# A transformer block on one core: first loads issued from two engines, first weight cast moved to VectorE, first matmuls in another order

## The chip, the cores and the metric

The kernel runs on one core of a Trainium2 chip. The core has a matmul engine (TensorE, "PE" in the profile, with its weight loads listed apart as "PEld"), VectorE ("DVE"), ScalarE ("ACT"), GpSimd ("POOL") and a queue engine ("SP") that issues most DMA transfers. ACT and POOL can issue transfers too. The metric is the time of one execution on the device in microseconds (us). Lower is better.

## The reference

One block on a sequence of 512 tokens with 1024 channels, float32. The input is normalised, projected by one wide matrix, and the projection feeds a convolution branch and a state-space branch; both are gated, mixed, normalised and followed by a gated feed-forward network:

```python
def reference(x, mix_pre_g, w_in, ...):
    h = rms_norm(x, mix_pre_g[i])
    proj = h @ w_in[i]
    u_glu = proj[..., :OFF_Z]
    z = proj[..., OFF_Z:OFF_XBC]
    xbc = proj[..., OFF_XBC:OFF_DT]
    dt_raw = proj[..., OFF_DT:OFF_GATE]
    gates = jax.nn.sigmoid(proj[..., OFF_GATE:] + gate_b[i])
    g_conv, g_ssm = jnp.split(gates, 2, axis=-1)
    conv_out = conformer_conv_branch(u_glu, ...)
    ssm_out = ssd_branch(z, xbc, dt_raw, ...)
    mixed = (g_conv * conv_out + g_ssm * ssm_out) @ w_out[i]
    x = x + rms_norm(mixed, mix_post_g[i])
    h = rms_norm(x, ffn_pre_g[i])
    gt, up = jnp.split(h @ w_gate_up[i], 2, axis=-1)
    f = (jax.nn.silu(gt) * up) @ w_down[i]
    x = x + rms_norm(f, ffn_post_g[i])
    return x
```

The change touches only the beginning: the first part of `h @ w_in`, whose columns `u_glu` are made of a half "val" and a half "glu".

## The kernel before, in words

Activations are held channel-major: a tile has 128 channels on the partitions and the 512 tokens along the free dimension, so that the 1024 channels are 8 k steps. Weights come in pieces of 128x1024 float32 (512 KB), each holding, for 128 output columns, the 8 k steps side by side, 128 columns per step.

**Split products.** To keep float32 precision, every operand is split into an upper and a lower part in the faster matmul format. For weights, `w_part` (line 167) first casts the raw piece to the upper part `whi` on ACT (L169), then takes the lower part `wlo = raw - whi` on DVE (L176), or for some later pieces through a DMA. For the input, `ehi` is the scaled input on ACT (L334) and `elo` the remainder on DVE (L325). A product is three matmuls: upper weight by upper input, lower weight by upper input, upper weight by lower input.

**The start.** While the first transfers are under way, PE runs 8 matmuls on a zeroed tile (`WARM = 8`, L293; each shows in the trace as two passes, 16 rows in all). ACT loads its function table and makes a one-column copy (`warm`, L290). SP issues all first transfers, in this order: `x0g` (the first 128 channels of the transposed input, with the gains beside it), the first quarter (256 columns, two k steps) of the weight pieces 0, 1 and 2 (`raw0`, `raw1`, `raw2`, L308), the second input tile `xT1`, the second quarters of the three pieces, `xT2`, `xT3`, the second halves of the three pieces, then `xT4` to `xT7` and whole pieces from there on. SP's transfers signal on 8 semaphores in turn; a transfer that comes round to a semaphore waits until the one before it on the same semaphore has landed.

**The first matmul group** (L514 to L518) makes three results at once, `pv0` (val 0), `pg0` (glu 0) and `pv1` (val 1), with one accumulator bank each. The loop runs over the 8 k steps, in each over the three results, and for each result over the three products:

```python
for k in range(NK):
    for ps, (wh, wl) in zip(three, ws):
        c = slice(k * P, (k + 1) * P)
        in_order(pe.matmul(ps, wh[:, c], ehi[k], start=k == 0, stop=False))
        pe.matmul(ps, wl[:, c], ehi[k], start=False, stop=False)
        mark["pe"] = pe.matmul(ps, wh[:, c], elo[k], start=False, stop=k == NK - 1)
```

k steps 0 and 1 need the first quarters of the weights, steps 2 and 3 the second quarters, steps 4 to 7 the halves. Beside this, ACT also squares each input tile (`sq`, L346) and DVE adds the squares (`ssq`, L347) for the norm, whose factor is applied to the first results later (`rb`).

**Order.** Instructions that are not tied by `in_order` are placed by a scheduler that works on its own estimates, so moving one changes its neighbours on ACT and DVE. Each engine then runs its own list strictly in that order, and waits on semaphores for the others. After the first group the kernel goes on for about a thousand microseconds with the other projections, the two branches, the mixing and the feed-forward network; nothing of that is touched.

## Time and profile before

| | |
|---|---|
| runs | 1023.64, 1025.57, 1022.51 us; median 1023.64 |
| the profiled execution | 1022.63 us, of which the span of the core's instructions is 1020.9 us |
| TensorE busy | 1007.8 us, 99% of the span |
| VectorE, ScalarE, GpSimd busy | 843.7, 616.6, 105.6 us |
| moved by DMA | 155.55 MB, 152 GB/s over the span |

Times in the views count from the start of the span. A row of the order of time gives the start, the time taken, engine, line, operation, output and inputs, and in brackets the idle time of the engine before it and what released it. "SPq" and "ACTq" are transfers being issued by SP and ACT. A matmul row's length includes the time through the array; back to back, the next starts before the last has ended, so the distance of their starts is what one costs.

### The profile page before, as it was taken

How to read it: one execution, taken by the hardware profiler on the slowest of the kernel's cores; microseconds unless marked ns; L12 is line 12 of the kernel's file. 1: busy time of each engine (PE TensorE's matmuls, PEld its weight loads, DVE VectorE, ACT ScalarE, POOL GpSimd, SP SyncE). 2: the span in 40 equal slices, each digit the busy share in tenths (PEclk: the TensorE clock that was granted, in tenths of full speed). 3: DMA queues.
4: the chain of work that ended last, by engine and by line, in shares of the span. 5: the costliest groups of instructions: out<-in, count | busy, mean ns of one | idle time of the engine just before them, and what ended most of it. 6: DMA issues, size and time to landing. Idle time of an engine off the chain costs nothing.

```text
span 1020.9 us, 15946 instructions
## 1 busy us (share of the span) xinstructions
PE 1007.8 (99%) x6181; PEld 881.9 (86%) x6181; DVE 843.7 (83%) x1227; ACT 616.6 (60%) x1034; POOL 105.6 (10%) x131
## 2 busy tenths in 40 slices
PE   9999999999999999999999999999999999999997
PEld 7898889888888888888888889889999999988885
DVE  7899977878696879578987889688998788799974
ACT  7645775667666656573552676466676565678542
POOL 0011202120121012101010110011000000001000
PEclk9999999999999999999999999999999999999999
DMA  8567645646554465455352455634656455469622
GB/s 287 157 161 197 185 101 145 182 99 170 148 150 118 128 183 145 113 148 153 81 145 64 123 177 134 221 106 128 207 145 191 120 145 160 129 192 294 196 83 83
DMA packets 44235, 155.55 MB, mean 152 GB/s; under 512 B 5120, under 2 KB 6144, under 8 KB 43136
## 3 DMA queue, kind: packets, MB, share of 16 engines
q1 hardware_dynamic: 30672, 104.66, 30.2%
q0 software_dynamic: 11280, 43.52, 21.8%
q10 hardware_dynamic: 2208, 6.36, 1.7%
q8 instruction: 48, 0.79, 0.3%
q14 instruction: 27, 0.22, 0.1%
HBM read 150.26 MB, written 4.26 MB: 151 GB/s over the span
## 4 chain that ended last, share of the span: by engine, by line
PE 88%; DVE 6%; ACT 2%; issue 1%; DMA 1%; SPq 0%; POOL 0%; ACTq 0%; DVEq 0%; POOLq 0%
PE xy L209 4%; PE xy L211 4%; PE xy L210 4%; PE pso L209 3%; PE pso L210 3%; PE pso L211 3%; PE pz L210 3%; PE pz L211 3%; PE px L211 2%; PE px L209 2%; PE px L210 2%; PE pz L209 2%; PE yv L209 2%; PE yv L210 2%; PE yv L211 2%
## 5 line engine op out<-in xcount | busy, mean ns | idle before, releaser
L467 DVE SCALAR_TENSOR_TENSOR a<-v,prm_t,a 128x511 f32<-128x511 f32 (+15 forms) x240 | 181.4, 759 | 15.5 <-ACT a L464 13.4
L169 ACT CAST whi<-raw 128x1024 fp32r<-128x1024 f32 (+2 forms) x108 | 106.8, 1000 | 131.1 <-PE pso L210 37.5
L176 DVE TENSOR_TENSOR wlo<-raw,whi 128x1024 fp32r<-128x1024 f32 (+2 forms) x67 | 74.9, 1123 | 38.3 <-ACT whi L169 37.6
L174 POOL DMA_DIRECT2D wlo<-in_w x41 | 36.5, 891 | 374.9 <-ACT wlo L173 121.0
L210 PE MATMUL pz<-wlo,hhi 128*128 128x512 f32 (+2 forms) x160 | 56.1, 351 | 0.4 <-DVE wlo L176 0.4
L211 PE MATMUL pz<-whi,hlo 128*128 128x512 f32 (+2 forms) x160 | 56.3, 352 | 0.0
L209 PE MATMUL pz<-whi,hhi 128*128 128x512 f32 (+2 forms) x160 | 55.4, 353 | 0.0
L209 PE MATMUL px<-hhi,whi 128*128 128x512 f32 x128 | 50.2, 392 | 0.0
L209 PE MATMUL pso<-yh,whi 128*128 128x512 f32 x128 | 50.0, 393 | 0.0
L211 PE MATMUL px<-hhi,wlo 128*128 128x512 f32 x128 | 49.8, 389 | 0.0
L210 PE MATMUL px<-hlo,whi 128*128 128x512 f32 x128 | 49.8, 389 | 0.0
L210 PE MATMUL pso<-yl,whi 128*128 128x512 f32 x128 | 49.7, 390 | 0.0
L211 PE MATMUL pso<-yh,wlo 128*128 128x512 f32 x128 | 49.7, 389 | 0.0
L1122 ACT CAST whi_g<-raw 128x1024 fp32r<-128x1024 f32 x40 | 41.3, 1051 | 11.9 <-DVE raw L1161 5.1
L551 DVE SCALAR_TENSOR_TENSOR x<-px,prm_t,x 128x511 f32<-128x511 f32 (+2 forms) x48 | 34.7, 741 | 13.8 <-ACT x L549 13.8
L1127 DVE TENSOR_TENSOR wlo_g<-raw,whi_g 128x1024 fp32r<-128x1024 f32 x34 | 41.1, 1220 | 4.6 <-ACT whi_g L1122 4.5
L173 ACT ACTIVATE wlo<-whi 128x1024 fp32r<-128x1024 f32 x41 | 43.3, 1055 | 0.3
L449 ACT ACTIVATE L<-L,nacs 128x128 f32<-128x128 f32 x128 | 38.8, 389 | 0.5 <-POOL L L442 0.4
L210 PEld LDWEIGHTS pz<-wlo,hhi 128*128 128x128 f32 x160 | 30.2, 188 | 4.5 <-DVE wlo L176 0.7
L209 PEld LDWEIGHTS pz<-whi,hhi 128*128 128x128 f32 x160 | 30.2, 189 | 3.8
L211 PEld LDWEIGHTS pz<-whi,hlo 128*128 128x128 f32 x160 | 30.2, 188 | 3.7
L1122 ACT CAST chi_g<-raw 128x1024 fp32r<-128x1024 f32 x24 | 24.9, 1054 | 10.7 <-DVE raw L1161 4.1
(749 smaller groups left out, 3439.5 us busy)
## 6 DMA issues: line engine op xcount, KB each, us to landing
raw<-in_w SPq DMA_DIRECT2D x182, 512.0 KB, 4.4
wlo<-in_w POOLq DMA_DIRECT2D x41, 512.0 KB, 6.6
L<-scr POOLq DMA_DIRECT2D x8, 1024.0 KB, 7.2
wlo_g<-in_w POOLq DMA_DIRECT2D x11, 512.0 KB, 6.6
clo_g<-in_w POOLq DMA_DIRECT2D x7, 512.0 KB, 5.8
pws<-in_w POOLq DMA_DIRECT2D x8, 256.0 KB, 5.6
pw_raws<-in_w SPq DMA_DIRECT2D x4, 512.0 KB, 6.1
xr<-in_x ACTq DMA_DIRECT2D x4, 512.0 KB, 4.6
```

Source lines behind the costliest of these rows:

```text
L169: act.copy(hi[:, c], src[:, c])
L173: act.activation(lo[:, c], hi[:, c].bitcast(F32), AF.Copy, scale=-1.0)
L174: mark["lo"] = pool.dma_start(lo[:, c], w[n][:, c].bitcast(F32R), accum_op=ALU.add)
L176: mark["wlo"] = dve.tensor_tensor(out=lo[:, c], in0=src[:, c], in1=hi[:, c].bitcast(F32), op=ALU.subtract)
L209: mark["pe"] = pe.matmul(ps, lh, rh, start=start, stop=False, skip_group_check=more)
L210: pe.matmul(ps, lh, rl, start=False, stop=False, skip_group_check=more)
L211: mark["pe3"] = pe.matmul(ps, ll, rh, start=False, stop=stop, skip_group_check=more)
L449: act.activation(L[:, h, c, :], L[:, h, c, :], AF.Exp, bias=nacs[:, c, HG * g + h : HG * g + h + 1])
L467: return dve.scalar_tensor_tensor(out=va[j][:, d:], in0=vs[j][:, : T - d], scalar=col("dw_w", j * KC + KC - 1 - d), in1=va[j][:, d:], op0= ...
L551: dve.scalar_tensor_tensor(out=a[:, d:], in0=ps[:, : T - d], scalar=col("ssm_w", i * KS + KS - 1 - d), in1=a[:, d:], op0=ALU.mult, op1=ALU ...
L1122: a_ = act.copy(hi, src)
L1127: d_ = dve.tensor_tensor(out=lo, in0=src, in1=hi.bitcast(F32), op=ALU.subtract)
```

## The change

- One warm-up matmul fewer (7 instead of 8).
- The first input tile `x0g` is loaded as two transfers, 64 partitions each, one issued by SP and one by ACT. The first quarter of `raw0` is issued by SP, those of `raw1` and `raw2` by ACT. The remaining first transfers stay on SP, in the order that they had. ACT issues its three transfers before it loads its function table.
- The upper part of the first quarter of weight piece 0 is cast on DVE instead of ACT.
- In k step 0 the three upper products (one per result) are issued first, then for each result the two others. The other k steps keep their order, all of it now fixed in program order.

```diff
-WARM = 8
+WARM = 7
...
-    def w_part(n, c):
+    def w_part(n, c, by_dve=False):
         (hi, lo), src = split[n], raws[n]
-        act.copy(hi[:, c], src[:, c])
+        if by_dve:
+            dve.tensor_copy(hi[:, c], src[:, c])
+        else:
+            act.copy(hi[:, c], src[:, c])
...
+    x0g = ssd.tile([P, 3 * GW], F32, tag="yo", name="x0g")
+    for n, (q, h) in enumerate(((nc.sync, slice(0, 64)), (nc.scalar, slice(64, P)))):
+        in_order(q.dma_start(x0g[h, : T + NK], x0[h]))
+    for n, q in enumerate((nc.sync, nc.scalar, nc.scalar)):
+        in_order(q.dma_start(raws[n][:, parts[0]], w[n][:, parts[0]]))
     warm = cp.tile([P, 1], F32, name="warm")
-    act.copy(warm, woken[:, :1])
+    in_order(act.copy(warm, woken[:, :1]))
...
-    def load(c):
-        for n in range(3):
-            in_order(nc.sync.dma_start(raws[n][:, c], w[n][:, c]))
-
-    for k in range(NK):
-        in_order(nc.sync.dma_start(xk[k] if k else x0g[:, : T + NK], xT[k] if k else x0))
-        if k == 0:
-            load(parts[0])
+    for k in range(1, NK):
+        in_order(nc.sync.dma_start(xk[k], xT[k]))
         if k in (1, 3):
-            load(parts[k + 1])
+            for n in range(3):
+                in_order(nc.sync.dma_start(raws[n][:, parts[k + 1]], w[n][:, parts[k + 1]]))
...
         if k in parts:
-            w_part(0, parts[k])
+            w_part(0, parts[k], k == 0)
...
             for k in range(NK):
+                c = slice(k * P, (k + 1) * P)
+                for n in range(3 if k == 0 else 0):
+                    in_order(pe.matmul(three[n], ws[n][0][:, c], ehi[k], start=True, stop=False))
                 for ps, (wh, wl) in zip(three, ws):
-                    c = slice(k * P, (k + 1) * P)
-                    in_order(pe.matmul(ps, wh[:, c], ehi[k], start=k == 0, stop=False))
-                    pe.matmul(ps, wl[:, c], ehi[k], start=False, stop=False)
-                    mark["pe"] = pe.matmul(ps, wh[:, c], elo[k], start=False, stop=k == NK - 1)
+                    if k:
+                        in_order(pe.matmul(ps, wh[:, c], ehi[k], start=False, stop=False))
+                    in_order(pe.matmul(ps, wl[:, c], ehi[k], start=False, stop=False))
+                    mark["pe"] = in_order(pe.matmul(ps, wh[:, c], elo[k], start=False, stop=k == NK - 1))
```

What stands on the engines is seen in three places. The first is SP's list from its beginning; the brackets name the semaphores that a transfer waits for, DMAHW0 to DMAHW7 being those that transfers signal. Before:

```order
L311 DMA x0g_106<-in_x0 128x520
L308 DMA raw0_124<-in_w 128x256
L308 DMA raw1_125<-in_w 128x256
L308 DMA raw2_126<-in_w 128x256
L311 DMA xT1_107<-in_xT 128x512
L308 DMA raw0_124<-in_w 128x256
L308 DMA raw1_125<-in_w 128x256
L308 DMA raw2_126<-in_w 128x256
L311 DMA xT2_108<-in_xT 128x512 [waits DMAHW0_49]
L311 DMA xT3_109<-in_xT 128x512 [waits DMAHW1_49]
```

And after:

```order
L298 DMA x0g_98<-in_x0 64x520
L300 DMA raw0_95<-in_w 128x256
L314 DMA xT1_114<-in_xT 128x512
L317 DMA raw0_95<-in_w 128x256
L317 DMA raw1_96<-in_w 128x256
L317 DMA raw2_97<-in_w 128x256 [waits DMAHW0_49]
L314 DMA xT2_115<-in_xT 128x512 [waits DMAHW1_49]
L314 DMA xT3_116<-in_xT 128x512 [waits DMAHW2_49]
```

Two transfers have left SP's list ahead of `xT1`. The lists of both engines share the 8 semaphores, so the second quarter of `raw2` now comes round to the semaphore of SP's half of `x0g` (DMAHW0) and `xT2` to that of ACT's half (DMAHW1).

The second place is ACT's list from its first cast or scaling of k step 0 on. Before (the table load and the one-column copy stand ahead of it):

```order
L334 ACTIVATE ehi0_114<-x0g_106 128x512
L169 CAST whi_0_152<-raw0_124 128x256
L169 CAST whi_1_154<-raw1_125 128x256
L169 CAST whi_2_158<-raw2_126 128x256
L334 ACTIVATE ehi1_115<-xT1_107,x0g_106 128x512
L169 CAST whi_0_152<-raw0_124 128x256
L346 ACTIVATE sq1_201<-xT1_107 128x512
L169 CAST whi_1_154<-raw1_125 128x256
L169 CAST whi_2_158<-raw2_126 128x256
L334 ACTIVATE ehi2_116<-xT2_108,x0g_106 128x512
```

And after (its half of `x0g` and the first quarter of `raw1` are issued ahead of this):

```order
L300 DMA raw2_97<-in_w 128x256
L302 ACT_TABLE_LOAD
L302 COPY warm_104<-woken_93 128x1
L336 ACTIVATE ehi0_121<-x0g_98 128x512
L172 CAST whi_1_154<-raw1_96 128x256
L172 CAST whi_2_158<-raw2_97 128x256
L336 ACTIVATE ehi1_122<-xT1_114,x0g_98 128x512
L172 CAST whi_0_152<-raw0_95 128x256
L172 CAST whi_1_154<-raw1_96 128x256
L172 CAST whi_2_158<-raw2_97 128x256
L348 ACTIVATE sq1_201<-xT1_114 128x512
L336 ACTIVATE ehi2_123<-xT2_115,x0g_98 128x512
```

The first cast has gone to DVE, and the square `sq1` has moved from between the casts of the second quarters to behind the last of them, directly ahead of `ehi2`. On DVE the moved cast stands first, ahead of `wlo` of piece 0; in DVE's later list two of the additions to `ssq` stand a place or two later.

The third place is PE's list in k step 0, behind the warm-up. Before:

```order
L516 MATMUL pv0_236<-ehi0_114,whi_0_152 128x512
L517 MATMUL pv0_236<-ehi0_114,wlo_0_153 128x512
L518 MATMUL pv0_236<-elo0_122,whi_0_152 128x512
L516 MATMUL pg0_237<-ehi0_114,whi_1_154 128x512
L517 MATMUL pg0_237<-ehi0_114,wlo_1_155 128x512
L518 MATMUL pg0_237<-elo0_122,whi_1_154 128x512
L516 MATMUL pv1_238<-ehi0_114,whi_2_158 128x512
```

And after:

```order
L518 MATMUL pv0_236<-ehi0_121,whi_0_152 128x512
L518 MATMUL pg0_237<-ehi0_121,whi_1_154 128x512
L518 MATMUL pv1_238<-ehi0_121,whi_2_158 128x512
L522 MATMUL pv0_236<-ehi0_121,wlo_0_153 128x512
L523 MATMUL pv0_236<-elo0_129,whi_0_152 128x512
L522 MATMUL pg0_237<-ehi0_121,wlo_1_155 128x512
L523 MATMUL pg0_237<-elo0_129,whi_1_154 128x512
```

The three upper products come first; from k step 1 on the list is the same as before.

More of the change, by code (lines that the diff above doesn't have):

```diff
@@ L293, in block_kernel @@
         in_order(pe.matmul(ps[:, :P], woken, woken, start=True, stop=True))
-    x0g = ssd.tile([P, 3 * GW], F32, tag="yo", name="x0g")
     pre_g = x0g[:, T : T + NK]
```

6 lines of the change are left out of this document (3 added, 3 removed).

## The prediction

> **What bounds the kernel now.** I read the page first, then what PE waits for, then PE's busy time by stretches, then the chain of waits through the first 12 us. The page's busy times and its chain:
>
> ```profile
> PE 1007.8 (99%) x6181; PEld 881.9 (86%) x6181; DVE 843.7 (83%) x1227; ACT 616.6 (60%) x1034; POOL 105.6 (10%) x131
> ...
> PE 88%; DVE 6%; ACT 2%; issue 1%; DMA 1%; SPq 0%; POOL 0%; ACTq 0%; DVEq 0%; POOLq 0%
> ```
>
> PE is busy 99% of the span, so a change at the start can gain only what PE loses at the start. PE's waits (total, times, longest, in us), and PE's busy time by stretches of the start (length, busy, instructions, clock, DMA share, GB/s):
>
> ```profile
> PE xy L209 <- DVE f L1315: 1.3, 1, 1.3
> PE pv L516 <- ACT ehi L334: 0.9, 1, 0.9
> ```
>
> ```profile
> 4.70:9.80 5.10, 5.02 (x19) 1.00 0.91 307
> 9.80:11.90 2.10, 1.15 (x4) 1.00 0.99 350
> 11.90:40.00 28.10, 28.10 (x134) 1.00 0.73 259
> ```
>
> The only wait of PE at the start, 0.9 us, is not in k step 0 but at 9.8 to 10.7, and behind 11.9 PE has no idle time for 28 us: there, an earlier start of PE would not be eaten by another wait. What the wait is made of, from the chain and the order of time:
>
> ```profile
> 4.48 5.42 DMA xT<-in_xT
> ```
>
> ```profile
> 9.27 0.41 ACT L169 CAST whi<-raw 128x256 fp32r<-128x256 f32 x1 [1.07 <-DMA raw<-in_w]
> ...
> 9.92 0.72 ACT L334 ACTIVATE ehi<-xT,x0g 128x512 fp32r<-128x512 f32 x1 [0.25 <-DMA xT<-in_xT]
> ...
> 10.67 0.75 DVE L325 SCALAR_TENSOR_TENSOR elo<-xT,x0g,ehi 128x512 fp32r<-128x512 f32 x1 [0.54 <-ACT ehi L334]
> ...
> 10.69 0.50 PE L516 MATMUL pv<-ehi,whi 128*128 128x512 f32 x1 [0.91 <-ACT ehi L334]
> ...
> 11.48 0.50 PE L518 MATMUL pv<-elo,whi 128*128 128x512 f32 x1
> ```
>
> This is k step 2. `xT2` lands at 9.90 (4.48 + 5.42), ACT scales it from 9.92, PE starts 0.77 us later (10.69), and `elo2`, hence the third product at 11.48, follows 1.56 us behind the start of `ehi2`. From there PE runs without a gap. So the end of the program moves with the start of `ehi2`, and everything that the change does to k steps 0 and 1 lies ahead of that wait. The quantity to work out is when ACT can start `ehi2`.
>
> **The change, part by part.** *Issue.* SP's issues before:
>
> ```profile
> 0.73 0.39 SPq L311 DMA_DIRECT2D x0g<-in_x  x1
> 1.17 1.37 SPq L308 DMA_DIRECT2D raw<-in_w  x3
> 2.58 0.43 SPq L311 DMA_DIRECT2D xT<-in_xT  x1
> 3.05 1.38 SPq L308 DMA_DIRECT2D raw<-in_w  x3
> 4.48 0.91 SPq L311 DMA_DIRECT2D xT<-in_xT  x2
> ```
>
> One issue costs about 0.47 us from start to start. With `raw1` and `raw2` gone to ACT, these two are issued 0.47 us earlier (at 1.17 and 1.64 behind ACT's half of `x0g`), `xT1` and the second quarters of `raw0` and `raw1` 0.94 us earlier. The second quarter of `raw2` would be issued at 3.06 instead of 4.00, but waits for SP's half of `x0g`; the whole of `x0g` landed by 3.67 (ACT's row below), so it is issued by 3.7, 0.3 earlier, and `xT2` by 4.15, also 0.3 earlier.
>
> *Landing.* An earlier issue is an earlier landing only where the transfers wait for the issue. The rate of all transfers from 1.6 to 5.6 us, in 40 slices of 0.1 us:
>
> ```profile
> GB/s 0 166 125 83 42 83 146 187 166 333 395 393 372 320 434 319 318 369 266 277 297 236 246 72 51 51 72 41 51 123 205 277 317 389 338 328 369 328 328 348
> ```
>
> From 3.9 to 4.5 six slices stand at 41 to 72, mean 56, against some 340 on both sides: the transfers have run dry there. That costs 0.6 x (1 - 56/340) = 0.50 us, and the three slices of climb behind it (123, 205, 277) another 0.12: 0.6 us in all. Behind it the rate is full, so `xT2`, 5.42 us under way, stood in line behind bytes. I take it that the earlier issues (0.47 and 0.94 us) fill this hole, so that all later landings come 0.6 us earlier. Unknown is how two issuing queues share the line; the nearest rows are two loads of the same size from either queue:
>
> ```profile
> raw<-in_w SPq DMA_DIRECT2D x182, 512.0 KB, 4.4
> ...
> xr<-in_x ACTq DMA_DIRECT2D x4, 512.0 KB, 4.6
> ```
>
> The ends: 0.2 us later (ACT's loads took 4.6 against 4.4), and 0.94 us earlier (the largest advance of an issue). I take 0.6, since the hole is measured and both advances that could fill it are of its size.
>
> Here stands the rule that speaks against this change. The Trainium skill (DMA: Bandwidth & Descriptors, Issuing engines are not separate DMA queues) says that transfers issued by different engines run on the same 16 DMA engines and interleave, and that only the issue time is saved; its Rules for kernel authors call two transfers to disjoint halves of the partitions not worth it. Taken at its word, splitting `x0g` gains nothing; the trace's hole agrees that issue time is what there is to save, and the case where even that saves nothing is the first rival below.
>
> *ACT.* Its rows at the start:
>
> ```profile
> 0.72 1.28 ACT L290 ACT_TABLE_LOAD   x1 [0.72 <-PEq L1703]
> 2.01 0.19 ACT L290 COPY warm<-woken 128x1 f32<-128x1 f32 x1
> 3.67 0.72 ACT L334 ACTIVATE ehi<-x0g 128x512 fp32r<-128x512 f32 x1 [1.46 <-DMA x0g<-in_x]
> 4.29 0.39 ACT L169 CAST whi<-raw 128x256 fp32r<-128x256 f32 x1
> 5.11 0.41 ACT L169 CAST whi<-raw 128x256 fp32r<-128x256 f32 x1 [0.43 <-DMA raw<-in_w]
> ...
> 6.97 0.39 ACT L169 CAST whi<-raw 128x256 fp32r<-128x256 f32 x1
> 7.27 0.63 ACT L346 ACTIVATE sq<-xT 128x512 f32<-128x512 f32 x1
> 7.80 0.39 ACT L169 CAST whi<-raw 128x256 fp32r<-128x256 f32 x1
> ```
>
> Three issues ahead of the table load take 3 x 0.47 = 1.41 us, so the table load and the copy end at about 3.6 instead of 2.2: just the 1.46 us that ACT idled there. It costs nothing unless `x0g` lands before 3.6; an earlier landing of its halves is then lost. The square that moved is the cost: ACT now does the last cast of the second quarters, then `sq1`, then `ehi2`. A cast costs 0.30 us from start to start (6.97 to 7.27), a square 0.53 (7.27 to 7.80). Before, the last cast waited for `raw2` until 9.27. So `ehi2` starts at the later of the landing of `xT2` and that of `raw2` + 0.83: with unmoved landings max(9.90, 10.10) = 10.10, 0.18 later than the 9.92 of before. With all landings 0.6 earlier it is 9.50, 0.42 earlier. That difference is the sum; the rest costs nothing:
>
> *The cast on DVE*:
>
> ```profile
> L176 DVE TENSOR_TENSOR wlo<-raw,whi 128x256 fp32r<-128x256 f32 x6 | 2.5, 423 | 4.8 <-ACT whi L169 4.8
> ```
>
> ```profile
> L361 DVE TENSOR_SCALAR dg<-ident,nrm 128x128 f32<-128x128 f32 x4 | 0.9, 284 | 1.3 <-POOL nrm L218 1.3
> ```
>
> No such cast of DVE is in the trace: between 0.28 us (one input, half the columns) and 0.42 (two inputs, the same columns); I take 0.4, the row with the same columns. DVE idles 4.8 us ahead of the six `wlo` of this stretch, which hides it. ACT is freed of 0.30 us before 5.11, where it waited for `raw1` anyway.
>
> *PE.* The warm-up's rows, a later product of the same 128x128 shape, and the first real ones and the first of k steps 3 and 4:
>
> ```profile
> L293 PE MATMUL warm_ps<-woken x16: 421/421/581, 1.0 to 4.4; 128*128 128x128 f32 x16
> ```
>
> ```profile
> L367 PE MATMUL prb<-dg,ones x8: 270/275/275, 31.8 to 32.6; 128*128 128x128 f32 x8
> ```
>
> ```profile
> 4.74 0.79 PE L516 MATMUL pv<-ehi,whi 128*128 128x512 f32 x1
> ...
> 6.20 0.39 PE L516 MATMUL pg<-ehi,whi 128*128 128x512 f32 x1
> ...
> 13.21 0.39 PE L516 MATMUL pv<-ehi,whi 128*128 128x512 f32 x1
> ...
> 15.25 0.39 PE L516 MATMUL pv<-ehi,whi 128*128 128x512 f32 x1
> ```
>
> One warm-up matmul is two passes of (4.4 - 1.0)/15 = 0.23: PE is free 0.45 us earlier, at about 4.3. `raw0` was there by 4.29, when ACT cast it without waiting, so DVE has `whi` of piece 0 by 4.7 at the latest, and `ehi0` ends at 4.39: the first product starts at about 4.6, 0.1 earlier, and the upper products fill the 1.46 us that stand between 4.74 and 6.20 with three products instead of the three of one result. All of that ends at k step 2: PE is done with k step 1 earlier and waits longer, about 1.1 us. With the wait at k step 2 gone, the whole of it would be worth at most the 0.45 us of the warm-up matmul. The norm's additions that moved on DVE end long before PE needs them:
>
> ```profile
> 23.35 0.69 DVE L347 TENSOR_TENSOR ssq<-ssq,sq 128x512 f32<-128x512 f32 x1
> ```
>
> ```profile
> L356 PEld LDWEIGHTS pss<-ones,ssq x8: 188/192/192, 25.9 to 26.8; 128*128 128x128 f32 x8
> ```
>
> 1.9 us lie between the last addition's end (24.04) and 25.9.
>
> The profiled execution took 1022.63 us, its span 1020.9; less 0.42 that is 1022.2. The median of the runs is 1.0 above it, so I predict 1023.64 - 0.42 = 1023.2.
>
> **The rivals.** *The landings don't move.* The line is limited by bytes, the hole only shifts. For it: the transfers run at 300 GB/s or more from 4.7 to 11.9, and `xT2` is late by bytes, not by issue. Against it: the hole. Then `sq1` ahead of `ehi2` decides: +0.18, time 1023.8, slower, on one ACT instruction, as soon as the landings come less than 0.18 us earlier. With ACT's loads 0.2 slower it is +0.38, 1024.0.
>
> *The issues bring their whole advance.* Landings 0.94 earlier: `ehi2` at 9.16, 0.76 earlier, time 1022.9. PE, done with k step 1 by about 9.3, would allow it. Against it: `raw2` and `xT2` are themselves issued only 0.3 earlier.
>
> *PE's slow start lasts longer.* The warm-up passes are 0.23 apart, those of `prb` (32.6 - 31.8)/7 = 0.11: PE runs at half rate at first, though the clock column says 1.00, and at full rate from 6.20. If k steps 0 and 1 all ran at half rate, 0.46 instead of 0.23 apart, 18 products from 4.6 would end at 12.9; a k step at full rate takes 2.04 (13.21 to 15.25), so k step 3 would start at 14.9 instead of 13.2: +1.7, time 1025.3. It decides from five half-rate products more than before (1.1 us of wait divided by 0.23). For it: one warm-up fewer. Against: PE's work has no gap over 0.2 us there, and products begin earlier. The Trainium skill (TensorE: Matmul & The Clock Gate, What's actually happening) says the full rate comes after about 3.4 us of sustained activity, in a free-running window, whatever the number of matmuls; by that rule PE gets its full rate at about the same time as before, and a step that misses a window would wait for the next, which is this rival.
>
> **How the numbers follow.** Forecast (landings 0.4 to 0.8 earlier) 0.60; landings not moved 0.22; whole advance 0.10; half rate 0.05; something unseen 0.03. What a measurement of this kernel can tell is about 0.3%, 3.1 us, the spread of the three runs shown. None of the cases reaches it, so: within 0.3% 0.94, slower 0.03 (half rate that lasts beyond k step 3), faster 0.03. The range takes the cases from -0.76 to +0.38 (1022.9 to 1024.0) and adds 1 us on each side, a third of the runs' spread, for a median of few runs: 1021.9 to 1025.0.
>
> **What would show it.** Right: no hole in the rate before 4.5; `ehi2` at about 9.5 with `sq1` just ahead of it; PE's wait at k step 2 longer than 0.9 us, its end at about 10.3; the first product at about 4.6; everything behind shifted by the same 0.4 us. Wrong: `ehi2` later than 9.92, a wait of PE behind k step 2 that was not there, matmuls 0.46 us apart behind 6.2, or ACT waiting for its own two weight quarters past 7.5 (it has 1.9 us there, since `ehi2` needs 2.4 us of ACT's work behind them).

## The result and the profile after

The changed kernel takes 1026.3 us (median of 20 runs, 1024.52 to 1031.67) against 1023.27 us for the kernel before in the same series (20 runs, 1021.47 to 1028.46): a ratio of 1.0031, 95% interval 1.0017 to 1.0045. It is slower by 0.3%, some 3 us; predicted were 1023.2 us and no measurable change. Two further series of the changed kernel gave ratios of 1.0010 [0.9994, 1.0025] and 1.0031 [1.0011, 1.0052] (`after_again` and `after_third` below). The profiled execution took 1025.14 us with a span of 1023.4, against 1022.63 and 1020.9 before: +2.5 us.

The times of every kernel here, the one before too, fall into two heaps some 5 us apart (the last section shows the stage that this comes from), and a median moves with the share of the upper heap. So beside each ratio stands the first quartile of the times less the first quartile of before in the same series, which the upper heap reaches least. For the changed kernel it is +2.75 us (1025.085 less 1022.333).

PE's busy time in the stretches that the prediction spoke of (length, busy, instructions, clock, DMA share, GB/s), after the change:

```profile
4.40:6.40 2.00, 0.00 (x0) 1.00 0.95 293
6.40:9.80 3.40, 3.38 (x8) 1.00 0.92 297
9.80:11.90 2.10, 2.10 (x6) 1.00 0.81 270
11.90:40.00 28.10, 28.10 (x132) 1.00 0.71 249
```

The same stretches of the kernel before:

```profile
4.40:6.40 2.00, 1.93 (x6) 1.00 0.92 305
6.40:9.80 3.40, 3.39 (x15) 1.00 0.87 292
9.80:11.90 2.10, 1.15 (x4) 1.00 0.99 350
```

Two things changed places. PE's idle time, 0.9 us at k step 2 before, is now 2.0 us ahead of the first product. And from 6.4 to 9.8, where PE is busy without a break in both, it gets through 8 products instead of 15: they run at half the rate. The clock column reads 1.00 in all of these rows, so it does not tell: in every trace here the clock records begin with the rise to full rate, and ahead of that record the column shows 1.00. The distance of the starts does tell. PE's own rows after the change:

```profile
6.42 0.77 PE L518 MATMUL pv<-ehi,whi 128*128 128x512 f32 x1 [2.02 <-DVE whi L170]
6.98 0.63 PE L518 MATMUL pg<-ehi,whi 128*128 128x512 f32 x1
...
10.40 0.63 PE L521 MATMUL pv<-ehi,whi 128*128 128x512 f32 x1
...
12.10 0.50 PE L522 MATMUL pg<-ehi,wlo 128*128 128x512 f32 x1
12.44 0.39 PE L523 MATMUL pg<-elo,whi 128*128 128x512 f32 x1
...
13.37 0.39 PE L521 MATMUL pv<-ehi,whi 128*128 128x512 f32 x1
```

From 6.98 to 12.10 the products are 0.43 us apart (12 steps in 5.12 us) and their rows 0.63 long; from 12.44 on they are 0.23 apart and 0.39 long. The last row is the first product of k step 2, which stood at 10.69 before, so PE is 2.68 us late there. The first product is 1.68 late (6.42 against 4.74). The 18 products of k steps 0 and 1 take 6.95 us (6.42 to 13.37), where before they took 5.95 with the wait at their end: 1.00 more. These two make up the 2.68. The norm's matmuls, later on the same engine, start in the kernel before and in the changed one at

```profile
L356 PE MATMUL pss<-ones,ssq x8: 168/250/250, 26.1 to 26.8; 128*128 128x1 f32 x8
```

```profile
L358 PE MATMUL pss<-ones,ssq x8: 169/250/251, 28.4 to 29.1; 128*128 128x1 f32 x8
```

that is 2.3 us later, and the span ends 2.5 us later. The rest of the 2.68 is time that k step 2 lost before and no longer loses: it took 2.52 us (10.69 to 13.21), with its third product waiting for `elo2` until 11.48, and now takes 2.06 (13.37 to 15.43). The norm's row serves below as the mark of what the start has cost. The code behind it is the same in all kernels, but its time is not: from this row to the first `yv` row of the last section it took 709.5 to 712.6 us in the twenty profiles. The mark moves too: two edits that cost nothing in the times, `order_only` and `x_halves`, have it at 25.5, against the 26.1 of the one profile of before. So half a microsecond at the mark of a single execution says little. The chain of waits of the changed kernel, in order of time, says what was late:

```profile
0.73 0.57 SPq L298
...
1.35 4.60 DMA raw<-in_w
...
5.98 0.31 DVE whi L170
...
6.42 0.77 PE pv L518
```

The first quarter of `raw0`, issued 0.18 us after where it stood before (1.35 against 1.17), was under way for 4.60 us and landed at 5.95. Before, ACT had cast it at 4.29. The chain no longer passes through `xT2`. On ACT and DVE one sees that k step 2 was ready long before PE was:

```profile
4.21 0.72 ACT L336 ACTIVATE ehi<-x0g 128x512 fp32r<-128x512 f32 x1 [0.30 <-DMA x0g<-in_x]
...
8.21 0.62 ACT L348 ACTIVATE sq<-xT 128x512 f32<-128x512 f32 x1
...
8.74 0.71 ACT L336 ACTIVATE ehi<-xT,x0g 128x512 fp32r<-128x512 f32 x1
...
9.65 0.75 DVE L327 SCALAR_TENSOR_TENSOR elo<-xT,x0g,ehi 128x512 fp32r<-128x512 f32 x1
```

`ehi2` starts at 8.74 instead of 9.92 and `elo2` ends at 10.40, while PE comes to k step 2 at 13.37. The quantity on which the prediction was built, the start of `ehi2`, improved by 1.18 us, more than the largest case, and no longer mattered.

### The profile page after: what moved, and what is told of

It is laid out like the page before. It is cut to its first block, busy times and chain, and to the rows that moved or that the text cites. A ratio compares the mean times of both kernels' runs of the same rounds, so it can differ in the third digit from the quotient of the medians.

```text
span 1023.4 us, 15945 instructions
## 1 busy us (share of the span) xinstructions
PE 1008.8 (99%) x6179; PEld 883.2 (86%) x6179; DVE 843.1 (82%) x1228; ACT 616.2 (60%) x1033; POOL 105.9 (10%) x131
## 4 chain that ended last, share of the span: by engine, by line
PE 93%; DVE 3%; DMA 1%; issue 1%; ACT 1%; POOL 0%; ACTq 0%; DVEq 0%; POOLq 0%; SPq 0%
PE xy L212 4%; PE xy L213 4%; PE xy L214 4%; PE pz L213 3%; PE pz L214 3%; PE pz L212 3%; PE pso L212 3%; PE pso L213 3%; PE px L214 3%; PE pso L214 3%; PE px L212 3%; PE px L213 3%; PE yv L213 2%; PE yv L212 2%; PE yv L214 2%; PE yd L664 2%
```

## The experiments

Each run is the kernel before or the changed kernel with the edit shown. "Rate up" below is the time of the clock record that puts PE at full rate.

**First series: which half of the change, and is it the warm-up?** Theory: PE starts late and cold, and runs at half rate for so long that PE itself becomes the bound. Rival: the loads are late, and the rate is beside the point.

`after_warm16`, the changed kernel with a long warm-up:

```diff
-WARM = 7
+WARM = 16
```

> The kernel after the change with 16 warm-up matmuls instead of 7, nothing else. Theory 1 (clock): the first weight quarter lands late, PE idles about 2 us behind the warm-up, and therefore runs its first products at half rate up to 12.1 us. With the warm-up reaching into the first product there is no idle time: products from about 6.6 us on at 0.23 us each, no stretch at 0.43, time about 1023 us, 3 us below the 1026.3 of the changed kernel. Theory 2 (landings): the late landings alone cost the time; the warm-up changes nothing, time about 1026 us.

Measured: 1023.97 us, ratio 1.0006 [0.9991, 1.0021], quartile +0.39. The rate was up at 4.02. The first product came at 6.04, but not for want of data: `raw0` had been cast from 4.45 on, and it was the warm-up that lasted until then. For `raw1` and `raw2`, which were late, PE waited 0.20 and 0.38 us. The norm's matmuls started at 26.4. So the longer warm-up alone takes back most of the loss; the 0.3 us left at the mark hold the late data and the length of the warm-up together.

`before_warm4`, the kernel before with a short warm-up (`WARM = 4`):

> The kernel before with 4 warm-up matmuls instead of 8, so that PE idles from about 2.8 us to the first product at 4.7. Theory 1 (clock): the idle time alone, without any change of the loads, brings the stretch at half rate; first products 0.43 us apart up to 9 or 12 us, time 1.5 to 2.5 us above the kernel before, 1025 to 1026. Theory 2 (landings): nothing changes, about 1023.3 us.

Measured: 1023.42 us, ratio 1.0012 [1.0002, 1.0023], quartile +0.62. PE stayed at half rate until 10.26, but the cost expected (1.5 to 2.5 us) did not come: the norm's matmuls started at 26.6, 0.5 late. PE came to k step 2 at 11.61, 0.92 later than before, and passed through it without the 0.46 us that it lost there before. So half rate alone costs little where the data of k step 2 are the bound.

`loads_only`, the changed loads with the rest as before:

```diff
-WARM = 7
+WARM = 8
...
-            w_part(0, parts[k], k == 0)
+            w_part(0, parts[k])
...
-                for n in range(3 if k == 0 else 0):
-                    in_order(pe.matmul(three[n], ws[n][0][:, c], ehi[k], start=True, stop=False))
```

(and the three products of a result one behind the other in k step 0 too).

> Of the change only the loads (two issuing engines, first x tile in halves); 8 warm-up matmuls, the first cast on ACT and the order of products as before. Both theories put the loss on the loads: the first quarter of piece 0 lands near 6 us instead of 4.3, time 2 to 3 us above the kernel before, 1025.3 to 1026.3. A third possibility, that the cast on DVE, the order of the products or the warm-up matmul cost the time, expects about 1023.3.

Measured: 1024.3 us, ratio 1.002 [1.0006, 1.0034], quartile +0.51. Expected were 2 to 3 us; the median stands 1.4 above that of before in its series (1024.3 against 1022.87). In the profile the first product came at 5.15, the rate was up at 5.65 and the norm's matmuls started at 25.5, so that this execution lost nothing at the start. What the loads cost in the other executions was not seen.

`no_loads`, the rest of the change (7 warm-up products, cast on DVE, upper products first) with the loads of before:

```diff
-WARM = 8
+WARM = 7
...
-        act.copy(hi[:, c], src[:, c])
+        if by_dve:
+            dve.tensor_copy(hi[:, c], src[:, c])
+        else:
+            act.copy(hi[:, c], src[:, c])
```

> The change without its loads: 7 warm-up matmuls, the first cast on DVE, upper products first, all first loads issued by SP as before. Theories 1 and 2: within 0.5 us of the kernel before, 1022.8 to 1023.6, first product near 4.7 us, PE still waits at k step 2. The third possibility: about 1026.

Measured: 1023.64 us, ratio 1.0012 [1.0001, 1.0024], quartile +0.66. Its profile shows the mechanism best. PE by stretches, and PE's rows:

```profile
4.00:7.20 3.20, 1.88 (x7) 1.00 0.81 256
7.30:10.60 3.30, 3.30 (x10) 0.54 0.92 309
10.70:14.00 3.30, 3.30 (x15) 0.96 1.05 404
```

```profile
4.38 0.50 PE L519 MATMUL pv<-ehi,whi 128*128 128x512 f32 x1
4.82 0.49 PE L519 MATMUL pg<-ehi,whi 128*128 128x512 f32 x1
6.57 0.50 PE L519 MATMUL pv<-ehi,whi 128*128 128x512 f32 x1 [1.26 <-ACT whi L172]
...
7.15 0.40 PE L524 MATMUL pv<-elo,whi 128*128 128x512 f32 x1
7.39 0.49 PE L523 MATMUL pg<-ehi,wlo 128*128 128x512 f32 x1
7.67 0.63 PE L524 MATMUL pg<-elo,whi 128*128 128x512 f32 x1
...
10.66 0.53 PE L523 MATMUL pg<-ehi,wlo 128*128 128x512 f32 x1
```

The rate was up at 4.12. Then the third upper product waited 1.26 us for `raw2`, the rate fell at 7.53, in the midst of PE's unbroken work, and came back at 10.95. Between these three points lie 3.41 and 3.42 us. The rows fit a rate that is decided at fixed points 3.41 us apart, by how full PE was in the stretch that has just ended (the last section counts this over all profiles); an idle time can then cost a whole such stretch at half rate, later, when nothing is late any more. The Trainium skill (TensorE: Matmul & The Clock Gate, What's actually happening) states such a free-running window of 3413 ns; the trace agrees. The norm's matmuls started at 26.9, 0.8 late, and the wait at k step 2 that was expected was not there: PE came to it at 11.96.

**Second series: which of the loads.** `after_again` is the changed kernel once more.

> The changed kernel once more, to see in a second execution what of its first 13 us repeats. Theory 1 (idle time of PE ahead of late data, then half rate): again a gap of 1 us or more behind the warm-up, and a stretch of products 0.43 us apart, but its length may differ (3 to 6 us), so that the norm's matmuls start between 27 and 29 us against 26.1 in the kernel before; time about 1026. Rival (the first profile was a chance): no gap, no such stretch, norm's matmuls near 26.

Measured: 1024.98 us, ratio 1.001 [0.9994, 1.0025], quartile +1.53; rate up at 10.54, norm's matmuls at 27.8. None of its 10 runs lay in the upper heap, against 9 of 35 of before, which draws the ratio down. The lateness is there again, in another place: the first product starts at 4.93 and PE then waits for the next weight piece:

```profile
PE pg L518 <- ACT whi L172: 1.4, 1, 1.4
```

`raw_act`: only `raw1` and `raw2` on ACT's queue, `x0g` whole on SP's, the rest as in `loads_only`:

```diff
-    for n, (q, h) in enumerate(((nc.sync, slice(0, 64)), (nc.scalar, slice(64, P)))):
-        in_order(q.dma_start(x0g[h, : T + NK], x0[h]))
+    in_order(nc.sync.dma_start(x0g[:, : T + NK], x0))
```

> Of the change only this: the first quarters of raw1 and raw2 are issued by ACT; x0g whole on SP, 8 warm-up matmuls, cast and product order as before. If the two engines' transfers share the line so that SP's first ones are held up: x0g lands after 3.7 and raw0 after 4.3 us, SP's issues take about 0.57 instead of 0.39 us; 0.5 to 1.5 us slower than before. If the halves of x0g are what costs, nothing here: 1022 to 1023.

Measured: 1023.61 us, ratio 1.0002 [0.9985, 1.0019], quartile +0.25. Here `x0g` itself is late. It is issued as before, and what is new is that two weight quarters are issued beside it:

```profile
0.73 0.39 SPq L297 DMA_DIRECT2D x0g<-in_x  x1
0.73 0.89 ACTq L299 DMA_DIRECT2D raw<-in_w  x2
1.17 0.42 SPq L299 DMA_DIRECT2D raw<-in_w  x1
...
4.70 0.72 ACT L335 ACTIVATE ehi<-x0g 128x512 fp32r<-128x512 f32 x1 [1.57 <-DMA x0g<-in_x]
```

against 3.67 before. PE waited 0.97 us for its first product, which came at 5.77. But the rate was up at 4.64, and the norm's matmuls started at 25.6: late data at full rate cost nothing at the mark here.

`x_halves`: only `x0g` in two halves, the three weight quarters on SP's queue, the rest as in `loads_only`:

```diff
-    for n, q in enumerate((nc.sync, nc.scalar, nc.scalar)):
+    for n, q in enumerate((nc.sync, nc.sync, nc.sync)):
```

> Of the change only this: x0g in two halves of the partitions, one issued by SP and one by ACT; raw0, raw1, raw2 all on SP. If the halves cost: x0g complete at 4.1 to 4.2 us instead of 3.6, time 0.3 to 1 us above before. If not: within 0.3 us of before. In both cases the second quarters are issued at the old times, so that k step 2 still waits as before.

Measured: 1023.07 us, ratio 0.9996 [0.9983, 1.0008], quartile -0.12. The halves bring nothing: `ehi0` started at 3.96, 0.29 later than with the whole tile.

`loads_warm16`, which is `loads_only` with `WARM = 16`:

> The loads of the change with 16 warm-up matmuls, the cast on ACT and the product order as before. Theory 1: without idle time of PE behind the warm-up no product runs at half rate, and the earlier second quarters and xT2 are gained: norm's matmuls at 25.5 to 26.0 us against 26.1 before, time 0.2 to 0.6 us below the kernel before, 1022.3 to 1022.7. Theory 2 (late landings alone): 1 to 1.5 us above, as with 8 warm-up matmuls.

Measured: 1023.41 us, ratio 0.9992 [0.9973, 1.0012], quartile -0.05. In its profile the rate was up only at 6.90, the warm-up lasted until the first product at 7.41, and PE waited for no data at all. That the norm's matmuls started at 26.6, 0.5 late, is thus not the cost of late data; it fits a warm-up that lasted too long. The gain that was expected (25.5 to 26.0) did not come.

**Third series: the order of the products.** `after_old_order` is the changed kernel with the three products of a result one behind the other in k step 0, as before:

```diff
-                c = slice(k * P, (k + 1) * P)
-                for n in range(3 if k == 0 else 0):
-                    in_order(pe.matmul(three[n], ws[n][0][:, c], ehi[k], start=True, stop=False))
                 for ps, (wh, wl) in zip(three, ws):
-                    if k:
-                        in_order(pe.matmul(ps, wh[:, c], ehi[k], start=False, stop=False))
-                    in_order(pe.matmul(ps, wl[:, c], ehi[k], start=False, stop=False))
-                    mark["pe"] = in_order(pe.matmul(ps, wh[:, c], elo[k], start=False, stop=k == NK - 1))
+                    c = slice(k * P, (k + 1) * P)
+                    in_order(pe.matmul(ps, wh[:, c], ehi[k], start=k == 0, stop=False))
+                    pe.matmul(ps, wl[:, c], ehi[k], start=False, stop=False)
+                    mark["pe"] = pe.matmul(ps, wh[:, c], elo[k], start=False, stop=k == NK - 1)
```

> The changed kernel with the products of k step 0 in the order of before (loads on two engines, cast on DVE and 7 warm-up matmuls kept). Theory A (the new order and the late weight quarters work together: PE stands at the second and third upper product until raw1 and raw2 land, and the idle time costs the full rate): here PE works through the three products of the first result while raw1 lands; wait of PE under 1 us in one piece, a shorter stretch at half rate or none, norm's matmuls at 25.5 to 26.8 us against 28.4 and 27.8 in the two executions of the changed kernel, time within 0.8 us of before. Theory B (loads and warm-up alone cost it): as the changed kernel, 2 us above before.

Measured: 1024.1 us, ratio 1.0012 [1.0, 1.0024], quartile +1.01. Its profile showed half rate until 10.61 and the norm's matmuls at 27.7, as in the changed kernel, but that execution, at 1025.51, was among the slowest three of twelve. The times spoke for a share of the order, the profile against it, and it was run again at the end.

`order_only`, the kernel before with the new order alone:

> Of the change only the product order of k step 0; loads by SP, cast on ACT, 8 warm-up matmuls. Theory A: PE waits for raw2 at the third upper product, about 0.5 to 1.3 us, which may cost some products at half rate; norm's matmuls at 26 to 27 us, time 0 to 0.8 us above before, clearly less than the whole change. If the order alone were the cause: 2 us above.

Measured: 1023.14 us, ratio 1.0001 [0.9989, 1.0012], quartile +0.26, norm's matmuls at 25.5. By itself the order costs nothing.

`after_warm9`, the changed kernel with `WARM = 9`:

> The changed kernel with 9 warm-up matmuls instead of 7, so that the warm-up ends near 4.9 us, about where the first product can start, but does not cover the wait for raw1 and raw2 behind it. Theory A: the later wait (1 us or more in k step 0) is still there and can still cost the full rate; time between that with 7 and that with 16 warm-up matmuls, 0.8 to 2 us above before. If the one warm-up matmul that was taken away were the cause: at or below before.

Measured: 1024.05 us, ratio 1.0004 [0.9991, 1.0016], quartile +0.87; rate up at 6.28, norm's matmuls at 25.7.

`before_warm12`, the kernel before with `WARM = 12`:

> The kernel before with 12 warm-up matmuls instead of 8, which reach past the first product's start (4.7 us). If before itself loses the full rate in some executions, this gains a few tenths of a us; PE has no idle time up to k step 2; norm's matmuls at 25.8 to 26.2 us; time 0 to 0.4 us below before. If not, no change, or up to 0.3 us lost because the warm-up delays the first products.

Measured: 1023.01 us, ratio 0.9994 [0.9977, 1.0011], quartile -0.06. Its profile is the shortest of all (span 1019.8, norm's matmuls at 25.1), its times are not: a longer warm-up than eight is no gain that can be measured.

**Fourth series: late data and half rate apart.** `after_third` is the changed kernel for the third time.

> The changed kernel once more, timed on the same chip as the three others of this call. By the window theory about two of three executions miss the early window (a window of 3.41 us must lie in the 3.35 us of warm-up up to about 0.6 us): full rate from 9 to 12.7 us on, norm's matmuls at 27 to 28.5; the third that meets it: full rate before 5 us, norm's matmuls near 26. Median 1.5 to 3 us above before.

Measured: 1026.25 us, ratio 1.0031 [1.0011, 1.0052], quartile +3.09; rate up at 12.60, norm's matmuls at 28.6. This time `raw0` was in time and `raw1` was late:

```profile
4.87 0.80 PE L518 MATMUL pv<-ehi,whi 128*128 128x512 f32 x1 [0.47 <-ACT ehi L336]
6.67 0.79 PE L518 MATMUL pg<-ehi,whi 128*128 128x512 f32 x1 [1.01 <-ACT whi L172]
```

`before_warm7`, the kernel before with `WARM = 7`, so that its data are in time and only the rate suffers:

> The kernel before with 7 warm-up matmuls. The data land at 4.7 us as before, so the warm-up's earlier end opens a gap of only 0.3 us. Window theory: full rate by 7.3 us at the latest, as before, time within 0.5 us of before. If the missing warm-up matmul alone were the cause: 1.5 us or more above.

Measured: 1022.88 us, ratio 0.9999 [0.9983, 1.0014], quartile +0.21. Full rate by 7.3 was expected, but one warm-up product fewer was enough here for half rate until 10.27:

```profile
4.63 0.80 PE L516 MATMUL pv<-ehi,whi 128*128 128x512 f32 x1 [0.23 <-ACT whi L169]
...
9.76 0.63 PE L518 MATMUL pv<-elo,whi 128*128 128x512 f32 x1
10.18 0.43 PE L516 MATMUL pg<-ehi,whi 128*128 128x512 f32 x1
```

It cost 0.5 us at the norm (26.6) and nothing measurable in the times; `before_warm4`, with the same rows from there on, stands just clear of 1 (1.0012 [1.0002, 1.0023]).

`after_warm12`, the changed kernel with `WARM = 12`, so that the data are late and the rate does not suffer:

> The changed kernel with 12 warm-up matmuls: busy from 1.0 to about 5.8 us, so that every phase of the window finds 85% of busy time by 7.3 us. Window theory: full rate no later than 7.3 us, norm's matmuls at 25.5 to 26.6, median 1 to 2.5 us below the changed kernel on this chip, within 0.8 us of before. Late data alone: as the changed kernel.

Measured: 1023.68 us, ratio 1.0005 [0.9987, 1.0023], quartile +0.41. PE waited for the second and third upper products at full rate,

```profile
PE pg L518 <- ACT whi L172: 0.8, 1, 0.8
PE pv L518 <- ACT whi L172: 0.2, 1, 0.2
```

and the norm's matmuls started at 26.5, 0.4 late. So each of the two by itself costs no more than 0.4 to 0.5 us at the mark, which is within what single executions differ by, and both together 1.7 to 2.5 (27.8, 28.4 and 28.6 against 26.1 in three profiles). The quartiles say the same: +0.21 and +0.41 against +1.5 to +3.1. That the two don't add up fits the slack of before: 0.91 us of wait ahead of k step 2 and 0.46 lost within it take up the one or the other, but not both. This is read from the rows and was not isolated.

`order_warm12`, the new order with `WARM = 12` and the loads of before, was the candidate for a faster kernel:

> The kernel before with the new product order in k step 0 and 12 warm-up matmuls; loads by SP, cast on ACT. Window theory: no idle time that matters, full rate by 7.3 us; norm's matmuls near 25.3 us, time 0 to 0.8 us below before, which the scatter of the later stages may hide.

Measured: 1022.92 us, ratio 1.0007 [0.9987, 1.0028], quartile +0.10. No version here beats the kernel before.

**Two last runs.** `after_warm8`, the changed kernel with `WARM = 8`:

> The changed kernel with the eight warm-up products of before. One product more ends the warm-up about 0.43 us later (about 4.8 us in the span), while the first real product comes at 4.9 to 6.5. If the gap between warm-up and first product (late data, 0.5 to 2 us) is what misses the faster rate, one product more is too little: half rate in most executions, the norm's matmuls at 27.5 to 28.5 us, ratio 1.001 to 1.003. If the one warm-up product that the change took away is itself the cause, the rate is up by about 6.5 us, the norm's matmuls start at 25.7 to 26.5 as with nine, and the ratio is 0.9995 to 1.0008.

Measured: 1026.3 us, ratio 1.0025 [1.0003, 1.0047], quartile +2.69. So the one warm-up product that the change dropped is not alone what it lost by; with eight the changed kernel is as slow. Yet the execution that was profiled was the fastest of its twelve, 1022.65 us, and there the rate was up at 4.67, right at the end of the warm-up:

```profile
5.67 0.47 PE L518 MATMUL pv<-ehi,whi 128*128 128x512 f32 x1 [0.87 <-DVE whi L170]
5.98 0.40 PE L518 MATMUL pg<-ehi,whi 128*128 128x512 f32 x1
```

With data almost as late as in the changed kernel, products 0.3 us apart from the first on and the norm's matmuls at 25.6, this one execution of the same program is 1.3 to 4.2 us faster than the six others of its lower heap (1023.98 to 1026.84). The rows fit this reading: when the decision falls differs from one execution to the next, and a warm-up of 7 or 8 products that is followed by an idle time brings the full rate only where one of the 3.41 us stretches happens to fall onto it.

`after_old_again` is `after_old_order` once more:

> The changed kernel with the product order of before, once more. Its first profile showed half rate to 10.6 us and the norm's matmuls at 27.7, but that execution, at 1025.5, was among the slowest of its kernel; the median of those below 1027 stood 0.8 us above that of before, where the changed kernel stands 1.9 to 2.7 above. If the order has a share (upper products first need raw1 and raw2 one product after raw0, and an execution in which they land late idles PE once more), the executions again lie 0.5 to 1.2 us above before, ratio 1.0005 to 1.0015, and the profile, if it shows the rate up before 7 us, has the norm's matmuls at 25.7 to 26.5. If the order has none, they lie 1.7 to 2.7 above, ratio 1.002 to 1.0035, and the norm's matmuls at 27.5 to 28.5.

Measured: 1026.99 us, with 6 of 12 runs in the upper heap; ratio 1.0013 [0.999, 1.0036], quartile +1.07 (+1.01 the first time). The rate was up at 8.96 and the norm's matmuls started at 26.4:

```profile
5.48 0.76 PE L518 MATMUL pv<-ehi,whi 128*128 128x512 f32 x1 [1.09 <-DVE whi L170]
6.04 0.63 PE L519 MATMUL pv<-ehi,wlo 128*128 128x512 f32 x1
```

With the old order the quartile stands 1.0 us above before, twice, and with the new one 1.5 to 3.1, three times. This speaks for a share of the order, though it costs nothing with the loads of before; `loads_only`, with the old order too, stands on the same side (+0.51). It doesn't show one for certain: the intervals of the ratios overlap ([1.0, 1.0024] and [0.999, 1.0036] with the old order, [0.9994, 1.0025] to [1.0017, 1.0045] with the new), and the quartile of one and the same kernel moved by 1.6 us between series. The rows agree with a reason: behind the first product the old order has two more that need only `raw0`, and PE goes on without a break, where the new order needs `raw1` next (1.01 us of wait in `after_third`, 1.35 in `after_again`). That these waits are the reason was not isolated.

The runs on which the verdict rests:

| kernel | data late | PE warm-up | ratio | quartile, us | rate up at, us | norm's matmuls at, us |
|---|---|---|---|---|---|---|
| before | no | 8 | | | 5.42 | 26.1 |
| `before_warm7` | no | 7 | 0.9999 | +0.21 | 10.27 | 26.6 |
| `after_warm12` | yes | 12 | 1.0005 | +0.41 | 5.28 | 26.5 |
| after | yes | 7 | 1.0031 | +2.75 | 12.33 | 28.4 |
| `after_again` | yes | 7 | 1.0010 | +1.53 | 10.54 | 27.8 |
| `after_third` | yes | 7 | 1.0031 | +3.09 | 12.60 | 28.6 |
| `after_warm8` | yes | 8 | 1.0025 | +2.69 | 4.67 (its fastest execution) | 25.6 |
| `after_old_again` | yes | 7, old order | 1.0013 | +1.07 | 8.96 | 26.4 |

With the data in time, or with a warm-up of 9 products or more, the ratios of the runs above lie between 0.9992 and 1.0012. With late data, the new order and 7 or 8 warm-up products the loss is 1.5 to 3.1 us at the quartile, in four series; with the old order in place of the new it is 0.2 to 1.1, in four (two of them, `raw_act` and `loads_only`, with eight warm-up products and the cast on ACT).

## Why the prediction was wrong, step by step

**What bounds the kernel.** The reading was right: the wait at k step 2 set the end, and behind it every microsecond that PE loses shows in the span (2.3 us at the norm, 2.5 at the end). That this wait was also the slack of PE's work ahead of it stands in the prediction only in its third rival, with 1.1 us; the sum gave PE's work ahead of it no loss at all.

**Issue: "one issue costs about 0.47 us".** Wrong for the halves of `x0g` and what is issued right behind them. The changed kernel's issues:

```profile
0.72 0.56 ACTq L298 DMA_DIRECT2D x0g<-in_x  x1
0.73 0.57 SPq L298 DMA_DIRECT2D x0g<-in_x  x1
...
1.32 1.08 ACTq L300 DMA_DIRECT2D raw<-in_w  x2
1.35 0.82 SPq L300 DMA_DIRECT2D raw<-in_w  x1
...
2.23 0.43 SPq L314 DMA_DIRECT2D xT<-in_xT  x1
```

Both engines took 0.57 us for half of `x0g`, where SP alone took 0.39 for the whole, and SP 0.82 for `raw0`, where three such issues had taken 1.37 together. `xT1` was issued 0.35 us earlier (2.23 against 2.58) and not 0.94. `x_halves` shows the same 0.57 on both engines, and 1.52 for the three quarters behind it. It is not that two engines issue at once: in `raw_act` they do, with `x0g` whole, and SP took 0.39 and 0.42 and ACT 0.89 for two. Why the halves take longer to issue was not tried.

**Landing: "all later landings come 0.6 us earlier".** This is the step that decided, and it failed in sign where it counted. The hole in the rate did close. The rate from 1.6 to 5.6 us after the change, in the same 40 slices:

```profile
GB/s 0 0 0 0 104 125 354 146 83 250 291 416 437 353 247 339 308 297 236 215 225 225 297 277 164 225 236 256 277 338 328 297 328 226 297 266 277 287 277 297
```

Between 3.9 and 4.5, where it was 41 to 72 GB/s, it is now 164 to 277. And the later tiles came earlier, by more than the 0.6 (`ehi2` by 1.18). But the hole was filled with the bytes of the later tiles, and over these 4 us only 0.96 MB moved, against 0.93 before. The first quarters now share the line with tiles that used to be issued behind them: `raw0` landed at 5.95 instead of by 4.29. By 5.6 us 0.96 MB had moved, while `x0g` and the three first quarters are 0.66 MB together, so some 0.3 MB of later tiles went ahead of the last bytes of `raw0`. `raw_act` shows the same of `x0g`, issued as before and a microsecond late. In other executions it was `raw1` or `raw2` that came late. Which one it was went mostly with the issues: where SP took 0.82 or 0.83 for `raw0`, it was `raw0` (the profile after, `after_old_order`, `after_warm8`); where SP took 0.57 and ACT 1.34 for its two, it was `raw1` or `raw2` (`after_again`, `after_third` and the runs with 9, 12 and 16 warm-up products), with `after_old_again` as the exception. The prediction moved all landings by one amount and never asked which of them PE needs first. The Trainium skill (DMA: Bandwidth & Descriptors, Issuing engines are not separate DMA queues) says that only the time of issuing is saved by a second engine; here not even that was saved in full (0.57 us for a half against 0.39 for the whole).

**ACT: "costs nothing unless `x0g` lands before 3.6".** The condition was right, the cost small: the table load now stands at 2.42, `ehi0` starts at 4.21 behind the late `x0g`, and 0.54 later than before. `sq1` stood directly ahead of `ehi2`, as forecast, and cost nothing. **The cast on DVE** took 0.29 us (forecast 0.4, bounds 0.28 and 0.42); it waited 4.99 us for its data, so where it is done does not matter.

**PE: "the first product starts at about 4.6", "PE's work has no gap over 0.2 us".** The warm-up ended at 4.40, about as forecast (4.3), but the first product started at 6.42, 4.93 and 4.87 in three profiles, with gaps of 2.02 us, or of 0.5 and then 1.0 to 1.4. The step failed because it took the landing of `raw0` (by 4.29) over from the kernel before, and with it the claim that PE's work has no gap.

**The rivals.** The third, half rate that lasts longer, is what happened: forecast were 0.46 us per product and 1.7 us lost at k step 3; measured were 0.43 and 1.7 to 2.5 us at the norm. It was given 0.05, because PE's work was to have no gap, and the late landing then opened one. Its sign stood in the prediction's own list: matmuls 0.46 us apart behind 6.2. It was treated as a thing of the warm-up's length, where the runs show that it takes the late data beside it: with the data in time, seven products cost nothing measurable (`before_warm7`), and with late data eight don't help (`after_warm8`). The other two rivals, about `ehi2`, were both overtaken: `ehi2` came earlier than in either, and did not gate.

**The numbers.** The range (1021.9 to 1025.0) ended below the 1025.3 of the prediction's own third rival. It missed the median of 1026.3 for two reasons: the loss of about 2 us, and the upper heap of the times, into which 8 of 20 runs fell here, against 3 of 20 of before. Whether the change has a part in the second is not known: over its three series the changed kernel had 12 of 42 runs above 1027, and the kernel before 17 of 90 above 1026.2, where its upper heap begins.

## What to carry to other kernels

When loads are issued earlier, ask of each landing whether it comes earlier or now shares the line with what was moved up behind it, and look first at the one that the busiest engine needs next. A wait in front of the bounding engine is also the slack of everything ahead of it: two costs that each fit into it can be free one by one and expensive together, so test them in pairs. Leave no idle time between PE's warm-up and its first real work, or let the warm-up last about as long as the data can be late: with 1.5 to 2 us of idle time there, the full rate came 5.6 to 7.7 us behind the first product in the three profiles of the changed kernel, while a warm-up of 16 products can outlast the data and become what PE waits for (`loads_warm16`).

## What the runs showed of the hardware that was not expected

**The rate is decided late, and differs between executions.** The times at which the rate changed are whole multiples of 3.41 us apart within one execution (4.12, 7.53, 10.95 in `no_loads`; 12.33 and the fall at the end, 1019.26, in the changed kernel, which are 295 times 3.4133 apart), but lie anywhere between executions. Counting 0.23 us for each pass of the warm-up and 0.43 us for each half-rate product, the stretch that ended with the rise in the kernel before (2.01 to 5.42) was about nine tenths full, and the one that ended without a rise in `before_warm7` (3.44 to 6.86) about three quarters. Counted in the same way, all twenty profiles agree: every stretch that ended with the first rise was at least 83% full (83% in `loads_only` and `after_warm16`), and every one ahead of it at most 76% (`after_old_order`). For the fall, counting 0.23 us for each product at full rate, the stretch from 4.12 to 7.53 in `no_loads` was 40% full and brought the rate down, while 44% in `raw_act` (4.64 to 8.05) and 47% in `after_warm8` (4.67 to 8.08) did not. These shares are estimates, worked out from the starts of the rows.

**Two paces of the same matmuls.** In the stage with 128x256 matmuls (730 to 905 us) PE is busy for all but 0.8 to 2.5 us, at one of two paces. The same tile in `order_only` and in `x_halves` (shortest, median and longest in ns, first and last start):

```profile
L209 PE MATMUL yv<-t1h,dhi x72: 276/276/277, 736.5 to 901.2; 128*128 128x256 f32 x72
```

```profile
L212 PE MATMUL yv<-t1h,dhi x72: 276/281/281, 735.5 to 906.1; 128*128 128x256 f32 x72
```

and PE in 20 us of that stage, of `order_only` and then of `x_halves`:

```profile
760.00:780.00 20.00, 20.00 (x179) 1.00 0.62 187
```

```profile
760.00:780.00 20.00, 20.00 (x172) 1.00 0.62 170
```

179 matmuls against 172 in the same time, with the same clock, and the stage ends some 5 us later (906.1 against 901.2, though it began 1.0 earlier). That is the distance of the two heaps of times, which the kernel before has too (1027.7 to 1028.5 in its own series). The three profiled executions above 1026.5 us (`x_halves` 1026.94, `loads_only` 1027.77, `after_old_again` 1028.94) have the slower pace as their median row, and the other seventeen the faster. What sets the pace was not tried.
